# The Silu gate of the mLSTM path moved behind the head-output transpose, with channels on partitions

## The chip, the cores and the metric

The kernel runs on one core of one Trainium2 chip. The metric is the device time in microseconds of one execution. Five engines of the core appear below: PE (TensorE, the matrix multiplier; PEld are its weight loads), DVE (VectorE), ACT (ScalarE), POOL (GpSimd) and SP (SyncE, which here only starts DMA transfers).

## The reference

One layer over 2048 tokens and 1024 model channels. RMSNorm, one input projection, two groups of heads, one output projection with a residual add, a final RMSNorm. The part that the change touches is the end of group A (4 heads of 256 channels):

```python
hm = mlstm_chunkwise(q, k, v, i_pre, f_pre)
hm = jax.nn.sigmoid(o_pre) * hm
hm = hm.reshape(B, S, N_HEADS, HEAD_DIM)
hm = hm * lax.rsqrt(jnp.mean(hm * hm, axis=-1, keepdims=True) + EPS)   # norm per token and head
hm = hm.reshape(B, S, D_MLSTM) * mh_norm_g                             # gain per channel
hm = hm * jax.nn.silu(z_m)                                             # gate per token and channel
mix = concatenate([hm, c])                    # c: convolution group, causal depthwise, width 31
h = h + einsum('bse,ed->bsd', mix, w_out)
```

So each element of the head output is multiplied by a factor of its token (the norm), a gain of its channel, and silu(z) of both. z = u W_z, where u is the normed input.

## The kernel before, in words

**Halves, units, heads, chunks.** The sequence is worked in two halves of 1024 tokens (`hf`). For each half the input projection is cut into *units* of 256 output channels. A unit is 8 steps over the 1024 input channels; every operand is split into a high and a low part, and three products (hh, hl, lh) are added, so that a unit is 8 x 3 products into four PSUM banks of the pool `gm` (five buffers). The units of a half come in this order: `g0, v0, g1, o0, z0, q0, k0`, then for each further head `g, g, v, o, z, q, k`, and at the end four `c` units. `g` feeds the convolution, `c` its gate, and `o`, `z`, `q`, `k`, `v` a head of the mLSTM.

**Two layouts of a unit.** Kind `fm` (L336) puts channels on partitions: the weights are the stationary operand, 512 tokens stream past, 96 matmuls of 512 columns. Kind `tm2` (L343) puts tokens on partitions: the activations are stationary, 256 channels stream, 192 matmuls of 256 columns. `q`, `k`, `g` and `c` are `fm`; `o`, `z` and `v` are `tm2`. What leaves PSUM must be multiplied by the norm factor of its token: in `tm2` a column `rstd["c"]` with one value per partition, in `fm` a row `rstd["b"]` of 512 values.

**Evacuation.** For each of the four banks of a `z` unit, and for each of its two token blocks, ACT takes a sigmoid (L450) and DVE multiplies it by the scaled value (L451): silu(z) with tokens on partitions, stored in `oz` beside the sigmoid of `o` (L438).

**The chunk chain.** After unit `k` of a head, `mlstm(hf, h)` puts that head's 8 chunks of 128 tokens into slots, one slot per step of the following units. A chunk has four parts. `s0`: `sk` on PE (scores and transposed k, in the only buffer of PSUM pool `tp`), `w` and `kw` on DVE and ACT, `qs` on DVE. `s1`: `num` on PE, state update `kv` on PE and `cs` on DVE, the denominator `dn` and `hm` (L694) on DVE, the sum of squares on ACT (L699), its power on POOL (L700). `s2`: second half of the state update; `hm` times norm factor times silu(z) on DVE (L706). `s3`: transpose of `hm` on PE (`mt`, L714, in the same single buffer of `tp`), channel gain on ACT (L719), and a DMA of `mo` to DRAM every second chunk.

**Background work.** The convolution is 31 taps over 1024 tokens for each of 8 blocks (L777 and L787 on DVE), put between other work by a credit counter (`pump`). The LayerNorm of the convolution runs in four blocks per half, those of half 0 at the beginning of half 1. A block has two matmuls on PE in its chain: `lm` for the mean and `lv` for the variance, then `bc_l` (broadcast), with DVE and ACT between them. The convolution's input tiles `c` have two buffers, so the PSUM bank of a `g` unit's first part (L756) can leave only after the convolution two blocks before is done.

**What sets the order.** Each engine runs its queue in order. The order of the queues is not the order of the code: a scheduler lays the program out by priorities and by its own estimate of times, and only the instructions marked with `keep_in_program_order` (the taps, the exponentials) are fixed. A change of a few operations therefore shifts matmuls and vector instructions in many places.

Of the kernel before, what the change touches and what calls it, by code (L numbers as in the profile page):

```python
# [14 lines left out]
F32 = mybir.dt.float32  # L15
F32R = mybir.dt.float32r
AF = mybir.ActivationFunctionType
ALU = mybir.AluOpType

P = 128  # L20
# [4 lines left out]
HD = 256  # L25
# [14 lines left out]
def hybrid_block_kernel(  # L40
# [12 lines left out]
    nc = tc.nc  # L53
# [5 lines left out]
    PAD, ODD = 8, 48  # L59
# [56 lines left out]
    def col(base, i):  # L116
        return vec[:, base + i : base + i + 1]
# [259 lines left out]
                pump(step_us * PUMP)  # L377


    q_t, k_t, v_t, oz_t = {}, {}, {}, {}  # L380
    gate = {}

    def ev_q(hf, h):
# [49 lines left out]

    def ev_o(hf, h):
        def f(i, ps):
            oz_t[h, i] = ozp.tile([P, 2, 2, HD], F32, tag="oz", name=f"oz_{hf}_{h}_{i}")
            for j in range(2):
                nc.scalar.activation(  # L438
                    oz_t[h, i][:, 0, j], ps[:, j * HD : (j + 1) * HD], AF.Sigmoid,
                    scale=rstd["c"][:, 2 * i + j : 2 * i + j + 1],  # L440
                )
        return f

    def ev_z(hf, h):
        def f(i, ps):
            t = oz_t[h, i]
            for j in range(2):
                pv = ps[:, j * HD : (j + 1) * HD]
                rc = rstd["c"][:, 2 * i + j : 2 * i + j + 1]
                nc.scalar.activation(t[:, 1, j], pv, AF.Sigmoid, scale=rc)  # L450
                nc.vector.scalar_tensor_tensor(  # L451
                    out=t[:, 1, j], in0=pv, scalar=rc, in1=t[:, 1, j], op0=ALU.mult, op1=ALU.mult
                )
        return f

    def gates(hf, gt):
# [103 lines left out]
    def mlstm(hf, h):  # L560
# [46 lines left out]
        def chunk(c):  # L607
# [4 lines left out]
            sl = slice(cc * P, (cc + 1) * P)  # L612
            last = hf == 1 and c == NCH - 1
            v = [v_t[h, c // 2][:, i, c % 2, :] for i in range(2)]
            sg = oz_t[h, c // 2][:, 0, c % 2, :]
            sz = oz_t[h, c // 2][:, 1, c % 2, :]
            t = {}

            def s0():
# [83 lines left out]
            def s2():  # L703
                state(1)
                hm = t["hm"][:, :HD]
                nc.vector.scalar_tensor_tensor(  # L706
                    out=hm, in0=hm, scalar=t["ss"], in1=sz, op0=ALU.mult, op1=ALU.mult
                )

            def s3():  # L710
                hm = t["hm"]
                mt = tp.tile([P, 512], F32, tag="tp", name=f"mt_{nm_}")
                for d in range(2):
                    nc.tensor.transpose(mt[:, d * P : (d + 1) * P], hm[:, d * P : (d + 1) * P], ident)  # L714
                if cc % 2 == 0:
                    dec["mo"] = k2p.tile([P, 2, 256], F32, tag="k2", name=f"mo_{nm_}")
                mo = dec["mo"]
                for d in range(2):
                    nc.scalar.activation(  # L719
                        mo[:, d, (cc % 2) * P : (cc % 2 + 1) * P], mt[:, d * P : (d + 1) * P],  # L720
                        AF.Identity, scale=col(V_MG, 2 * h + d),
                    )
                if cc % 2 == 1:
                    nc.sync.dma_start(
                        mixs[2 * hf + tb][:, 2 * h : 2 * h + 2, (cc - 1) * P : (cc + 1) * P], mo
                    )
# [194 lines left out]
    for hf in range(2):  # L921
        s = [("g", 0)]
        for h in range(NH):
            s += [("v", h)] + ([("g", 1)] if h == 0 else []) + [("o", h), ("z", h), ("q", h), ("k", h)]
            if h < 3:
                s += [("g", 2 * h + 2), ("g", 2 * h + 3)]
        s += [("c", j) for j in range(4)]
        seq.append(s)
        for u in s:
            if u == ("v", 0):  # L930
                for _ in range(2):
                    for g in range(2):
                        wsrc.append((wv0[g], 528, 0))
            else:
                for g in range(2):
                    wsrc.append((wu[WID[u], g], 512, ODD if u[0] in "ozv" else 0))
    for b in range(4):
        for nn in range(2):
            for g in range(8):
# [18 lines left out]
    for hf in range(2):  # L958
# [8 lines left out]
        for ui, (nm, i) in enumerate(s):  # L967
# [10 lines left out]
            if nm == "g":  # L978
                unit("fm", 8, 2, 256, opnd, ev_glu(hf, i), hook=hook)
            elif nm == "c":  # L980
                unit("fm", 8, 2, 256, opnd, ev_zc(hf, i), hook=hook)
            elif nm == "q":
                unit("fm", 8, 2, 256, opnd, ev_q(hf, i), hook=hook)
            elif nm == "k":
                unit("fm", 8, 2, 256, opnd, ev_k(hf, i), hook=hook)
                mlstm(hf, i)
            elif nm == "o":
                unit("tm2", 8, 2, 256, opnd, ev_o(hf, i), hook=hook)
            elif nm == "z":
                unit("tm2", 8, 2, 256, opnd, ev_z(hf, i), hook=hook)  # L990
            elif i > 0:
                unit("tm2", 8, 2, 256, opnd, ev_v(hf, i), hook=hook)
            else:
                for g in range(2):
                    unit("tm", 8, 2, 264, opnd, ev_v0(hf, g, gt), step_us=1.35, toks=[4 * g + i for i in range(4)])
                gq.append([0, gates(hf, gt)])
                gate_step()
# [129 lines left out]
```

## Time and profile before

| | |
|---|---|
| median of 3 runs | 2007.02 us (2005.82 to 2014.35) |
| the profiled execution's own time | 2014.07 us |
| its span in the profile | 2012.4 us |
| PE busy | 1975.9 us, 98% |
| DVE busy | 1445.4 us, 72% |
| ACT busy | 827.7 us, 41% |
| POOL busy | 792.3 us, 39% |
| granted PE clock, mean | 0.993 |

The profiled execution is one of the slower ones, 7 us above the median. PE is nearly always busy, so the first question is what each stretch of PE costs; the second is where PE does wait, and for whom. Busy time is an average: DVE's 72% is made of stretches near 95% and of a last fifth of the span below 35%. Rows of the trace that carry the argument stand in a section below. In them `start us, us` is the start and the length of a run of equal instructions; an entry in brackets is the idle time of the engine before it and who ended it. The four projections by layout: L336 is `fm`, L343 is `tm2`, L350 is the output projection and the first `v` unit.

### The profile page before, as it was taken

How to read it: one execution, taken by the hardware profiler on the slowest of the kernel's cores; microseconds unless marked ns; L12 is line 12 of the kernel's file. 1: busy time of each engine (PE TensorE's matmuls, PEld its weight loads, DVE VectorE, ACT ScalarE, POOL GpSimd, SP SyncE). 2: the span in 40 equal slices, each digit the busy share in tenths (PEclk: the TensorE clock that was granted, in tenths of full speed). 3: DMA queues.
4: the chain of work that ended last, by engine and by line, in shares of the span. 5: the costliest groups of instructions: out<-in, count | busy, mean ns of one | idle time of the engine just before them, and what ended most of it. 6: DMA issues, size and time to landing. Idle time of an engine off the chain costs nothing.

```text
span 2012.4 us, 29602 instructions
## 1 busy us (share of the span) xinstructions
PE 1975.9 (98%) x11562; PEld 1744.7 (87%) x11562; DVE 1445.4 (72%) x1915; ACT 827.7 (41%) x1703; POOL 792.3 (39%) x740
## 2 busy tenths in 40 slices
PE   8999999999999999999999999999999999999998
PEld 7998998899899888888889879988998887788887
DVE  6598887699679765557799998977896658733221
ACT  5233432442343246545345224424523555543332
POOL 4632432333243332433333324333432236565564
PEclk9999999999999999999999999999999999999999
DMA  4121121212122233335211211211221566766452
GB/s 151 64 69 53 58 74 43 63 49 74 42 69 74 74 110 125 113 126 162 85 53 53 69 42 59 74 53 53 64 74 53 163 220 200 248 231 231 155 190 95
DMA packets 85836, 204.10 MB, mean 101 GB/s; under 512 B 7296, under 2 KB 40256, under 8 KB 85696
## 3 DMA queue, kind: packets, MB, share of 16 engines
q1 hardware_dynamic: 85696, 202.21, 30.6%
q8 instruction: 91, 1.49, 0.3%
q14 instruction: 49, 0.40, 0.1%
HBM read 159.15 MB, written 43.03 MB: 100 GB/s over the span
## 4 chain that ended last, share of the span: by engine, by line
PE 73%; DVE 18%; DMA 3%; issue 2%; ACT 2%; POOL 0%; SPq 0%; POOLq 0%; DVEq 0%; ACTq 0%
PE gm L336 32%; PE gm L343 18%; PE gm L350 16%; DVE y L787 11%; PE num L601 3%; PE kv L601 2%; PE sk L627 1%; DMA ly<-ysc 1%; DVE sm L302 1%; DMA wr<-in_wo 1%; PE mt L714 1%; DVE ly L844 1%; DMA ysc<-y 1%; PE sk L631 1%; ACT ly L881 0%
## 5 line engine op out<-in xcount | busy, mean ns | idle before, releaser
L222 POOL TENSOR_TENSOR w<-wr,w 128x512 fp32r<-128x512 f32 (+1 forms) x392 | 603.1, 1543 | 878.2 <-ACT w L221 859.4
L336 PE MATMUL gm<-u_u,w 128*128 128x512 f32 x3840 | 908.6, 392 | 0.7 <-DVE u_u L293 0.6
L336 PEld LDWEIGHTS gm<-u_u,w 128*128 128x128 f32 x3840 | 712.5, 188 | 143.2 <-DVE u_u L293 1.3
L787 DVE SCALAR_TENSOR_TENSOR y<-c,vec,y 128x1024 f32<-128x1024 f32 x480 | 714.5, 1489 | 9.7
L343 PE MATMUL gm<-w,u_u 128*128 128x256 f32 x4224 | 521.9, 281 | 5.7 <-DVE oz L451 3.4
L343 PEld LDWEIGHTS gm<-w,u_u 128*128 128x128 f32 x4224 | 505.8, 190 | 7.6 <-DVE oz L451 3.6
L221 ACT CAST w<-wr 128x512 fp32r<-128x512 f32 (+1 forms) x392 | 241.4, 620 | 591.6 <-PE gm L336 200.2
L350 PE MATMUL gm<-w,u_m 128*128 128x512 f32 x1536 | 355.0, 392 | 3.1 <-POOL w L222 1.9
L350 PEld LDWEIGHTS gm<-w,u_m 128*128 128x128 f32 x1536 | 289.1, 189 | 64.2 <-POOL w L222 2.8
L281 DVE TENSOR_TENSOR u_m<-mr,u_m 128x1024 fp32r<-128x1024 f32 x32 | 47.2, 1475 | 77.7 <-ACT u_m L280 77.7
L1019 DVE TENSOR_TENSOR ht<-gm,ht 128x512 f32<-128x512 f32 x32 | 21.5, 687 | 112.2 <-PE gm L350 112.2
L700 POOL TENSOR_TENSOR ss<-ss,nhalf 128x1 f32<-128x1 f32 x64 | 55.5, 867 | 111.9 <-ACT sq L699 111.3
L633 DVE SCALAR_TENSOR_TENSOR w<-sk,rs,ee 128x128 f32<-128x128 f32 x64 | 22.0, 344 | 81.6 <-PE sk L631 79.1
L601 PE MATMUL kv<-v,kw 128*128 128x258 f32 x360 | 74.3, 291 | 0.6 <-DVE cs L666 0.4
L666 DVE SCALAR_TENSOR_TENSOR cs<-cs,g_so,kv 128x258 f32<-128x258 f32 x112 | 53.3, 476 | 25.1 <-PE kv L601 24.7
L639 ACT ACTIVATE kw<-sk,g_wa 128x256 fp32r<-128x256 f32 x60 | 28.3, 472 | 81.7 <-DVE w L633 81.6
L719 ACT ACTIVATE mo<-mt,vec 128x128 f32<-128x128 f32 x128 | 39.7, 362 | 52.3 <-PE mt L714 52.1
L601 PEld LDWEIGHTS kv<-v,kw 128*128 128x128 f32 x360 | 56.9, 190 | 3.2 <-DVE cs L666 0.6
L408 DVE SCALAR_TENSOR_TENSOR v<-gm,rs,v 128x256 fp32r<-128x256 f32 x64 | 29.5, 475 | 33.4 <-ACT v L407 33.4
L699 ACT ACTIVATE sq<-hm 128x257 bf16<-128x257 f32 x64 | 26.9, 420 | 64.6 <-DVE hm L694 64.4
L761 POOL TENSOR_TENSOR c<-c,g 128x512 f32<-128x512 f32 x32 | 40.9, 1284 | 30.4 <-ACT g L760 27.6
L350 PE MATMUL gm<-w,u_u 128*128 128x264 f32 x384 | 50.8, 294 | 0.0
(200 smaller groups left out, 1818.0 us busy)
## 6 DMA issues: line engine op xcount, KB each, us to landing
wr<-in_wu SPq DMA_DIRECT2D x123, 512.0 KB, 3.6
wr<-in_wo SPq DMA_DIRECT2D x64, 512.0 KB, 3.6
mr<-mixs SPq DMA_DIRECT2D x32, 512.0 KB, 4.6
ysc<-y SPq DMA_DIRECT2D x16, 512.0 KB, 2.6
mixs<-mo SPq DMA_DIRECT2D x32, 256.0 KB, 2.1
zsc<-zc SPq DMA_DIRECT2D x32, 256.0 KB, 2.1
ly<-ysc SPq DMA_DIRECT2D x16, 512.0 KB, 5.2
lz<-zsc SPq DMA_DIRECT2D x16, 512.0 KB, 6.0
```

What stands on the lines that cost most here:

```text
L221: nc.scalar.copy(hi, s)
L222: nc.gpsimd.tensor_tensor(out=lo, in0=s, in1=hi.bitcast(F32), op=ALU.subtract)
L281: nc.vector.tensor_tensor(out=l_, in0=src, in1=h_.bitcast(F32), op=ALU.subtract)
L336: nc.tensor.matmul(ps[i], wt[:, o + cb * P : o + (cb + 1) * P], at[:, tb * 512 : (tb + 1) * 512], start=st, stop=sp_,)
L343: nc.tensor.matmul(ps[i][:, t2 * 256 : (t2 + 1) * 256], at[:, t * P : (t + 1) * P], wt[:, o : o + ncol], start=st and t2 == 0, stop=sp_, s ...
L350: nc.tensor.matmul(ps[i][:, :ncol], at[:, t * P : (t + 1) * P], wt[:, o : o + ncol], start=st, stop=sp_,)
L601: nc.tensor.matmul(ps, x_, y_, start=start and i == 0, stop=stop and i == 2)
L666: nc.vector.scalar_tensor_tensor(out=cs[:, d], in0=cs[:, d], scalar=so[:, h, c : c + 1], in1=kv[:, :VW], op0=ALU.mult, op1=ALU.add,)
L700: nc.gpsimd.tensor_tensor(out=ss, in0=ss, in1=nhalf[:, 0:1], op=ALU.pow)
L719: nc.scalar.activation(mo[:, d, (cc % 2) * P : (cc % 2 + 1) * P], mt[:, d * P : (d + 1) * P], AF.Identity, scale=col(V_MG, 2 * h + d),)
L761: nc.gpsimd.tensor_tensor(out=c[:, sl], in0=c[:, sl], in1=g, op=ALU.mult)
L787: tc.keep_in_program_order(nc.vector.scalar_tensor_tensor(out=y, in0=c[:, j + i * H2 : j + (i + 1) * H2], scalar=col(V_CW, b * CW + j), in1=y,
```

## The change

`z` becomes an `fm` unit: 96 matmuls of 512 columns in place of 192 of 256. Its four banks are each left by one DVE multiplication with the row of norm factors (new L451) and one ACT Silu in SBUF (new L452). The tiles of `o` and `z` are separated; there are again four buffers, two for `o` and two for `z` of a head. In the chunk, `s2` is now an ACT scaling by the norm factor of the token (new L705, an Identity activation with a scale per partition), and `s3` multiplies gain and silu(z) on DVE as the transposed head output leaves PSUM (new L716, two instructions of 128 columns). The weights of `z` lose their 48-element offset in the weight tile.

```diff
-    q_t, k_t, v_t, oz_t = {}, {}, {}, {}
+    q_t, k_t, v_t, o_t, z_t = {}, {}, {}, {}, {}
...
     def ev_o(hf, h):
         def f(i, ps):
-            oz_t[h, i] = ozp.tile([P, 2, 2, HD], F32, tag="oz", name=f"oz_{hf}_{h}_{i}")
+            if i % 2 == 0:
+                o_t[h, i // 2] = ozp.tile([P, 4, HD], F32, tag="oz", name=f"o_{hf}_{h}_{i // 2}")
             for j in range(2):
                 nc.scalar.activation(
-                    oz_t[h, i][:, 0, j], ps[:, j * HD : (j + 1) * HD], AF.Sigmoid,
+                    o_t[h, i // 2][:, 2 * (i % 2) + j], ps[:, j * HD : (j + 1) * HD], AF.Sigmoid,
                     scale=rstd["c"][:, 2 * i + j : 2 * i + j + 1],
                 )
...
     def ev_z(hf, h):
         def f(i, ps):
-            t = oz_t[h, i]
-            for j in range(2):
-                pv = ps[:, j * HD : (j + 1) * HD]
-                rc = rstd["c"][:, 2 * i + j : 2 * i + j + 1]
-                nc.scalar.activation(t[:, 1, j], pv, AF.Sigmoid, scale=rc)
-                nc.vector.scalar_tensor_tensor(
-                    out=t[:, 1, j], in0=pv, scalar=rc, in1=t[:, 1, j], op0=ALU.mult, op1=ALU.mult
-                )
+            cb, tb = i % 2, i // 2
+            if cb == 0:
+                z_t[h, tb] = ozp.tile([P, 2, 512], F32, tag="oz", name=f"z_{hf}_{h}_{tb}")
+            t = z_t[h, tb][:, cb, :]
+            nc.vector.tensor_tensor(out=t, in0=ps, in1=rstd["b"][:, tb * 512 : (tb + 1) * 512], op=ALU.mult)
+            nc.scalar.activation(t, t, AF.Silu)
         return f
...
-            sg = oz_t[h, c // 2][:, 0, c % 2, :]
-            sz = oz_t[h, c // 2][:, 1, c % 2, :]
+            sg = o_t[h, tb][:, cc, :]
+            sz = z_t[h, tb][:, :, sl]
...
             def s2():
                 state(1)
                 hm = t["hm"][:, :HD]
-                nc.vector.scalar_tensor_tensor(
-                    out=hm, in0=hm, scalar=t["ss"], in1=sz, op0=ALU.mult, op1=ALU.mult
-                )
+                nc.scalar.activation(hm, hm, AF.Identity, scale=t["ss"])
...
                 for d in range(2):
-                    nc.scalar.activation(
-                        mo[:, d, (cc % 2) * P : (cc % 2 + 1) * P], mt[:, d * P : (d + 1) * P],
-                        AF.Identity, scale=col(V_MG, 2 * h + d),
+                    nc.vector.scalar_tensor_tensor(
+                        out=mo[:, d, (cc % 2) * P : (cc % 2 + 1) * P], in0=mt[:, d * P : (d + 1) * P],
+                        scalar=col(V_MG, 2 * h + d), in1=sz[:, d], op0=ALU.mult, op1=ALU.mult,
                     )
...
-                    wsrc.append((wu[WID[u], g], 512, ODD if u[0] in "ozv" else 0))
+                    wsrc.append((wu[WID[u], g], 512, ODD if u[0] in "ov" else 0))
...
             elif nm == "z":
-                unit("tm2", 8, 2, 256, opnd, ev_z(hf, i), hook=hook)
+                unit("fm", 8, 2, 256, opnd, ev_z(hf, i), hook=hook)
```

The scheduler moves instructions on every engine. Three places in the queues follow. They all lie at the start of half 1: the four LayerNorm blocks of half 0, then the first convolution blocks and the chunks of head 0. In the names the second number of `num_0_2` is the chunk, the last number of a name only tells equal names apart.

**PE, the variance matmul of the last LayerNorm block** (`lv_3`; `gm_0_9560` and `gm_x_904x` belong to unit `k0`). Before:

```order
L336 MATMUL gm_2_9431<-u_u_7_8131,w_9433 128x512 x3
L336 MATMUL gm_3_9432<-u_u_7_8131,w_9433 128x512 x3
L336 MATMUL gm_0_9560<-u_u_0_7963,w_9464 128x512
L859 MATMUL lv_3_9181<-invd,lq_3_0_9068 128x1 x2
L336 MATMUL gm_0_9560<-u_u_0_7963,w_9464 128x512 x2
```

Now, in the changed kernel:

```order
L336 MATMUL gm_1_9041<-u_u_6_7680,w_9044 128x512 x2
L336 MATMUL gm_2_9042<-u_u_0_7547,w_8944 128x512 x3
L336 MATMUL gm_2_9042<-u_u_1_7577,w_8944 128x512
L336 MATMUL gm_3_9043<-u_u_0_7547,w_8944 128x512 x3
L856 MATMUL lv_3_8751<-invd,lq_3_0_8652 128x1 x2
L336 MATMUL gm_2_9042<-u_u_1_7577,w_8944 128x512 x2
```

`lv_3` stood behind the first matmul of unit `k0`; it now stands behind 51 of its 96 (24 into the first bank, 20 into the second, 4 and 3 into the others).

**PE, chunks 2 and 3 of head 0** (`gm_3_10009` is the last bank of the unit `g3`). Before:

```order
L601 MATMUL num_0_2_10025<-c1h_0_1_9963,qssl_0_2_9955 128x258
L336 MATMUL gm_3_10009<-u_u_0_7963,w_9762 128x512 x3
L336 MATMUL gm_3_10009<-u_u_1_7993,w_9762 128x512 x3
L336 MATMUL gm_3_10009<-u_u_2_8012,w_9854 128x512 x3
L336 MATMUL gm_3_10009<-u_u_3_8034,w_9854 128x512 x3
L336 MATMUL gm_3_10009<-u_u_4_8053,w_9921 128x512 x3
L336 MATMUL gm_3_10009<-u_u_5_8077,w_9921 128x512 x3
L627 MATMUL sk_0_3_10070<-q_0_0_9554,k_0_0_9685 128x128 x2
L631 MATMUL sk_0_3_10070<-ident,k_0_0_9685 128x128 x2
L601 MATMUL kv_0_2_1_10091<-v_0_1_8417,kw_0_2_9944 128x258 x3
L336 MATMUL gm_3_10009<-u_u_6_8096,w_10010 128x512 x3
```

Now:

```order
L600 MATMUL num_0_2_9505<-c1h_0_1_9443,qssl_0_2_9435 128x258
L626 MATMUL sk_0_3_9550<-q_0_0_9034,k_0_0_9165 128x128 x2
L630 MATMUL sk_0_3_9550<-ident,k_0_0_9165 128x128 x2
L600 MATMUL kv_0_2_1_9571<-v_0_1_8001,kw_0_2_9424 128x258 x3
L600 MATMUL num_0_3_9618<-v_0_1_8001,wsh_0_3_9560 128x258 x2
L600 MATMUL kv_0_3_0_9628<-v_0_1_8001,kw_0_3_9557 128x258 x2
L711 MATMUL mt_0_2_9599<-ident,hm_0_2_9528 128x128 x2
```

Before, the matmuls of the last bank of `g3` and the beginning of the next unit lay between `sk` and `num` of chunk 3; now nothing but the three `kv` matmuls does, and that bank of `g3` comes after them.

**DVE, the same place** (`y` are taps of the convolution; `w_0_3` comes from `sk` of chunk 3). Before:

```order
L787 SCALAR_TENSOR_TENSOR y_0_9330<-c_0_8280,vec,y_0_9330 128x1024
L592 TENSOR_TENSOR qssl_0_2_9955<-qs_0_2_9952,qssh_0_2_9954 128x256
L756 TENSOR_TENSOR c_2_9994<-gm_2_9707,rb_8138 128x512
L756 TENSOR_TENSOR c_2_9994<-gm_0_9705,rb_8138 128x512
L666 SCALAR_TENSOR_TENSOR cs_0_9691<-cs_0_9691,g_so_9227,kv_0_2_0_10035 128x258
L687 TENSOR_SCALAR dn_0_2_10044<-num_0_2_10025,g_en_9223 128x1
L690 TENSOR_TENSOR dn_0_2_10044<-dn_0_2_10044,num_0_2_10025 128x1
L592 TENSOR_TENSOR c0l_0_2_10041<-cs_0_9691,c0h_0_2_10040 128x258
```

Now:

```order
L591 TENSOR_TENSOR qssl_0_2_9435<-qs_0_2_9432,qssh_0_2_9434 128x256
L716 SCALAR_TENSOR_TENSOR mo_0_0_9352<-mt_0_1_9461,vec,z_0_0_8899 128x128 x2
L665 SCALAR_TENSOR_TENSOR cs_0_9171<-cs_0_9171,g_so_8785,kv_0_2_0_9515 128x258
L784 SCALAR_TENSOR_TENSOR y_0_8852<-c_0_7864,vec,y_0_8852 128x1024
L686 TENSOR_SCALAR dn_0_2_9524<-num_0_2_9505,g_en_8781 128x1
L591 TENSOR_TENSOR c0l_0_2_9521<-cs_0_9171,c0h_0_2_9520 128x258
L665 SCALAR_TENSOR_TENSOR cs_0_9171<-cs_0_9171,g_so_8785,kv_0_2_1_9571 128x258
L784 SCALAR_TENSOR_TENSOR y_0_8852<-c_0_7864,vec,y_0_8852 128x1024
L689 TENSOR_TENSOR dn_0_2_9524<-dn_0_2_9524,num_0_2_9505 128x1
L591 TENSOR_TENSOR c1l_0_2_9577<-cs_0_9171,c1h_0_2_9576 128x258
L784 SCALAR_TENSOR_TENSOR y_0_8852<-c_0_7864,vec,y_0_8852 128x1024
L690 RECIPROCAL dn_0_2_9524<-dn_0_2_9524 128x1
```

The product `mo`, which leaves PSUM from the transpose, is new on DVE. Behind the last row shown follow a tap, `hm`, a tap and then `w_0_3`: five taps lie between `mo` of chunk 1 and `w` of chunk 3, and the two evacuations `c_2`, which free banks for `g3`, come five rows behind `w_0_3`. Before, `c_2` stood ahead of that.

## Rows read from the trace of the kernel before

**Rows 1.** The page's chain of work that ended last, by engine and by line.

```profile
PE 73%; DVE 18%; DMA 3%; issue 2%; ACT 2%; POOL 0%; SPq 0%; POOLq 0%; DVEq 0%; ACTq 0%
PE gm L336 32%; PE gm L343 18%; PE gm L350 16%; DVE y L787 11%; PE num L601 3%; PE kv L601 2%; PE sk L627 1%; DMA ly<-ysc 1%; DVE sm L302 1%; DMA wr<-in_wo 1%; PE mt L714 1%; DVE ly L844 1%; DMA ysc<-y 1%; PE sk L631 1%; ACT ly L881 0%
```

**Rows 2.** Windows: stretch, length; busy PE, PEld, DVE, ACT, POOL; clock, DMA.

```profile
300.00:400.00 100.00, 100.00 (x512) 85.26 (x511) 72.43 (x92) 33.72 (x72) 31.52 (x28) 1.00 0.19 58
...
976.00:1244.00 268.00, 256.67 (x1536) 227.14 (x1535) 252.21 (x324) 103.10 (x231) 94.13 (x87) 0.98 0.18 58
```

**Rows 3.** Windows of three z units, L343 alone: PE, PEld, clock.

```profile
285.83:307.75 21.92, 21.85 (x193) 21.65 (x192) 1.00 0.22 73
460.50:483.28 22.78, 22.76 (x194) 22.56 (x192) 1.00 0.21 70
...
906.00:937.30 31.30, 27.13 (x195) 25.74 (x194) 0.89 0.54 167
```

**Rows 4.** The same for one fm unit, L336 alone.

```profile
504.90:526.82 21.92, 21.92 (x98) 18.20 (x97) 1.00 0.16 49
```

**Rows 5.** PE in order of time, inside the z unit of half 1, head 0.

```profile
928.26 5.92 PE L343 MATMUL gm<-w,u_u 128*128 128x256 f32 x26 [3.42 <-DVE oz L451]
```

**Rows 6.** The window after that wait, as rows 2.

```profile
927.60:934.40 6.80, 6.14 (x29) 6.14 (x29) 2.41 (x6) 1.22 (x3) 1.28 (x1) 0.50 0.61 206
```

**Rows 7.** PE in order of time, lv_3 within unit k0 of half 1.

```profile
961.27 0.50 PE L859 MATMUL lv<-invd,lq 128*128 128x1 f32 x4
```

**Rows 8.** DVE in order of time, from lv_3 to the first chunks.

```profile
961.81 0.16 DVE L861 TENSOR_SCALAR lrs<-lv 128x2 f32<-128x2 f32 x1 [3.69 <-PE lv L859]
...
975.88 1.79 DVE L777 TENSOR_SCALAR y<-c,vec 128x1024 f32<-128x1024 f32 x1
977.71 15.00 DVE L787 SCALAR_TENSOR_TENSOR y<-c,vec,y 128x1024 f32<-128x1024 f32 x10
...
1025.39 0.48 DVE L694 SCALAR_TENSOR_TENSOR hm<-num,dn,oz 128x256 f32<-128x256 f32 x1
...
1060.01 0.22 DVE L687 TENSOR_SCALAR dn<-num,g_en 128x1 f32<-128x1 f32 x1 [0.72 <-PE num L601]
```

**Rows 9.** DVE by line and form: count, busy, mean ns, idle before, releaser.

```profile
L706 DVE SCALAR_TENSOR_TENSOR hm<-hm,ss,oz 128x256 f32<-128x256 f32 x64 | 36.6, 573 | 13.0 <-POOL ss L700 12.8
...
L451 DVE SCALAR_TENSOR_TENSOR oz<-gm,rs,oz 128x256 f32<-128x256 f32 x64 | 27.3, 476 | 2.4 <-ACT oz L450 2.1
...
L633 DVE SCALAR_TENSOR_TENSOR w<-sk,rs,ee 128x128 f32<-128x128 f32 x64 | 22.0, 344 | 81.6 <-PE sk L631 79.1 <-ACT sq L699 1.6 <-ACT ee L623 0.7
...
L807 DVE TENSOR_TENSOR zc<-gm,rb 128x512 f32<-128x512 f32 x32 | 21.3, 685 | 4.2 <-PE gm L336 2.0 <-DMA zsc<-zc 2.0
```

**Rows 10.** ACT by line and form.

```profile
L719 ACT ACTIVATE mo<-mt,vec 128x128 f32<-128x128 f32 x128 | 39.7, 362 | 52.3 <-PE mt L714 52.1
...
L450 ACT ACTIVATE oz<-gm,rs 128x256 f32<-128x256 f32 x64 | 27.9, 478 | 37.6 <-PE gm L343 23.4 <-DVE oz L451 14.2
...
L808 ACT ACTIVATE zc<-zc 128x512 f32<-128x512 f32 x32 | 19.2, 626 | 5.6 <-DVE zc L807 4.1 <-issue 1.4
...
L760 ACT ACT_TABLE_LOAD x13 | 16.7, 1283 | 2.1 <-DVE g L759 1.9
```

**Rows 11.** ACT in order of time, around a table load.

```profile
892.60 1.28 ACT L881 ACT_TABLE_LOAD   x1
893.90 4.05 ACT L881 ACTIVATE ly<-ly,vec 128x256 f32<-128x256 f32 x8
```

**Rows 12.** POOL by line, the power of the norm factor.

```profile
L700 POOL TENSOR_TENSOR ss<-ss,nhalf 128x1 f32<-128x1 f32 x64 | 55.5, 867 | 111.9 <-ACT sq L699 111.3
```

**Rows 13.** PE in order of time, waits in the stretch of rows 2.

```profile
998.78 0.39 PE L601 MATMUL num<-c0h_i,qssl 128*128 128x258 f32 x1 [0.90 <-DVE qssl L592]
...
1016.07 0.28 PE L601 MATMUL num<-c1h,qssl 128*128 128x258 f32 x1
...
1191.44 0.58 PE L601 MATMUL num<-c0h_i,qssl 128*128 128x258 f32 x1 [2.46 <-DVE qssl L592]
```

## The prediction

> **What bounds the kernel now.** I read the chain that ended last first. 73% of it is PE, most of that the three projection lines; 18% is DVE, and the largest share of that, 11%, is the taps of the convolution [rows 1]. So PE bounds the kernel, except in some stretch where the taps do. The windows say where. In an ordinary stretch (300 to 400) PE is busy for all 100 us and DVE for 72. From 976 to 1244 DVE is busy for 252.21 of 268 us, PE for 256.67 [rows 2]: both are nearly full, and which of them is late decides what a change is worth there. In order of time DVE starts its first tap at 975.88, and from then on it runs taps without a wait; the `num` matmul of a chunk starts at 1016.07 and lasts 0.28 us, and `hm`, which reads it, starts on DVE at 1025.39, 9 us later [rows 8, 13]. PE waits in this stretch are short and end with DVE (0.90 and 2.46 us, the shortest and the longest of those that I use) [rows 13]. I take DVE as the bound from 976 to 1244, and PE outside it.
>
> I then read PE's own cost of the units. A `z` unit in `tm2` takes 21.92 us in one window and 22.78 in another [rows 3]; four units (at 460, 635, 1290 and 1465) have the longer form. An `fm` unit takes 21.92 [rows 4]. The `z` unit of half 1, head 0 is a case of its own: its window is 31.30 us, at a mean clock of 0.89 [rows 3]. PE stands there for 3.42 us behind an evacuation on DVE [rows 5], and right after that wait 6.14 us of matmuls run at a clock of 0.50, which is 1.2 instead of 2.4 GHz [rows 6].
>
> **Part 1, z as an fm unit.** 96 matmuls of 512 columns replace 192 of 256. Seven of the eight units are ordinary. For the four longer ones PE gains 22.78 - 21.92 = 0.86 us each, for the others I take nothing. Two of the four lie before 976 and two after 1244: -1.7 and -1.7 us. The head-0 unit of half 1 should lose its 3.42 us wait, since its bank now leaves in one step of DVE that stands early in the queue and in front of ACT instead of behind it; with the wait the half clock goes, worth half of 6.14, so 3.07; and 0.86 as above. That is -7.35, with 0 as the other end (the evacuation again late behind other work of DVE).
>
> [...]
>
> **Part 2, evacuation.** Before, each bank costs DVE two instructions of 476 ns and ACT two of 478 [rows 9, 10]. Now DVE has one of 128x512 out of PSUM with a row, as the convolution gate does in 685 ns, and ACT one of 512 in SBUF, as that gate does in 626 [rows 9, 10]. Per unit DVE: 4 x 685 - 8 x 476 = -1.07 us; ACT: 4 x 626 - 8 x 478 = -1.3 us. ACT is hidden, being idle for 59% of the span, and for 165 of the 268 us in the dense stretch [rows 2].
>
> **Part 3, the chunk.** DVE loses `hm` x norm x silu, 573 ns [rows 9], and gets two products of 128x128 from PSUM. The nearest row is `w`, the same operation and shape from PSUM, 344 [rows 9]; as ends I keep 238 (half of the 256-column form) and 476. 2 x 344 - 573 = +115 ns a chunk (-97 to +379). ACT loses two instructions of 362 and gets one of 256 columns in SBUF, between 313 (half of the 512-column form) and 478 [rows 10]; at 420 it is 0.3 us lighter a chunk. The new wait: ACT's scaling needs the power from POOL, 867 ns [rows 12], for which DVE waited before. Behind it in ACT's queue stand mostly the high parts of `qs`, which lead to `num` on PE. If POOL were late each time, 64 x 0.87 = 56 us of ACT would stand; mostly an exponential and other casts lie between, and ACT has the room, so I cost it at nothing on the path, with 16 x 0.87 x a quarter = 3.5 us for the dense stretch as the upper end. PE now waits, for the single `tp` buffer, for DVE's products in place of ACT's: where DVE is late `mt` leaves later, and the next `sk` with it. DVE is in turn asked to wait for PE's `mt`. The one row of that kind shown is 0.72 us [rows 8]; I take +1 us for the dense stretch, 0 to 4.
>
> The dense stretch holds 16 chunks and one `z` unit: 16 x 0.115 - 1.07 = +0.8 us of DVE, +1 of waits, together +1.8.
>
> **Part 4, table loads.** ACT's queue holds 85 loads where it held 67, since Silu shares no table with its neighbours: 18 x 1.283 = 23.1 us on ACT [rows 10], hidden by the same idle time. After a load the next function starts 0.02 us later [rows 11].
>
> The Trainium skill speaks against this price: the page "ScalarE: Activation LUTs", section "What ACT_TABLE_LOAD costs", puts some 1380 ns of draining beside the 1283, 2.66 us a switch. By it 18 loads cost ACT 48 us. No drain is seen in the rows on either side of the load, so the trace does not agree; the forecast would be the same by both.
>
> **Part 5, the moved matmul.** This is the largest term. The last LayerNorm block of half 0 has its variance `lv_3` on PE; DVE waited 3.69 us for it and went on at 961.81 [rows 7, 8], then did the block's chain and began the taps at 975.88 [rows 8]. In the changed queue `lv_3` stands behind 51 of the 96 matmuls of `k0`, where it stood behind one. 50 x 21.92/96 [rows 4] = +11.4 us later. What precedes it on PE is 1.7 + 7.35 us earlier. So the first tap should start at 975.88 - 9.05 + 11.4, some 2.4 us later than before, and with it the stretch that DVE sets. The gain of parts 1 and 2 ahead of 976 is thus spent. DVE's row of waits [rows 8] names nothing else it could do meanwhile, since the taps keep their order; at best a part of the 15.8 us in which DVE is idle within the dense stretch [rows 2] makes up for it, and I put the lower end there at a third, -5 us.
>
> **Sum.** -1.7 - 7.35 + 11.4 + 1.8 - 1.7 = +2.4 us. On the profiled execution's own 2014.07 that is 2016.5; that execution was 7.05 above the median of 2007.02, so the time that I name is 2007.02 + 2.4 = 2009.4. Its own range: down by the 5 us of idle and a further 3 if all other units gain 0.86; up by 7.35 if the wait in `z` comes back: 2001 to 2017.
>
> **Rival A, PE sets the dense stretch.** PE is busy for 256.67 us of it and DVE for less, 252.21 [rows 2]. If the taps catch up before 1244, the later `lv_3` costs nothing and PE keeps all it saved: -1.7 - 7.35 - 0.86 (head 1) - 1.7 = -11.6, so 1995.4. For it: the busy times. Against it: `hm` 9 us behind `num`, and waits of PE that end with DVE [rows 8, 13].
>
> **Rival B, slower: chunk 3 stands on PE.** In the changed queue only three `kv` matmuls lie between `sk` and `num` of chunk 3 of head 0, where the last bank of `g3` and the next unit lay before. Meanwhile DVE has some five taps of 1.5 us (15.00 for ten [rows 8]) and small steps up to `w_0_3`: PE would stand for about 9 us. After the 3.42 us wait PE ran at half clock and lost 3.07 [rows 5, 6]; here as much. If DVE has taps enough to work through while PE stands, the 9 us are slack of PE and cost nothing, which is why they are not in the sum. They decide from the point where DVE itself runs dry, because the next chunk's `w`, `dn` and `hm` come from the matmuls that stand: then nothing of either engine's work covers them. DVE's idle time in the stretch, 15.8 us, of which 0.72 is a wait of that kind [rows 2, 8], leaves that open. Then +12.1 on the forecast: 2021.5.
>
> **Rival C, table loads on the path.** If each of the 18 loads stood ahead of something that PE waits for, +23 us: 2032. ACT ends few of the waits and is idle for most of the dense stretch [rows 2], so this is unlikely.
>
> **How the numbers follow.** Forecast 0.56, A 0.22, B 0.18, C 0.04. A measurement of this kernel can tell about 0.5%, some 10 us, from no change: below 1997 is faster, above 2017 slower. The forecast's own range touches neither; A is faster, B and C are slower. Faster 0.22, same 0.57, slower 0.21. The range goes to A and B, 1995 to 2021.5, and leaves out C and the outer part of either.
>
> **What would show it.** Part 1: `z` units of 21.9 us in windows at full clock, and no wait of some 3 us in the one of half 1, head 0. Parts 2 and 3: new lines on DVE near 685 and 344 ns, on ACT near 626 and 420; an idle entry of the scaling released by POOL would show the new wait. Part 5: `lv_3` in the middle of `k0`, and the first long run of taps near 978; a first tap well before 975 would refute the term. DVE again over 94% busy between there and the end of head 1's units bears out the forecast; PE without waits and DVE with idle time there speak for A; a PE wait of some 9 us at `num` of chunk 3, with a clock of 0.50 behind it and the end of the stretch 12 us late, for B. It would be wrong altogether if the time left 2001 to 2017.

## The result, and the profile after

The changed kernel takes 2030.12 us (median of 6, 2027.06 to 2030.83), the kernel before 2008.53 in the same runs: a ratio of 1.0102, interval 1.0091 to 1.0113. That is 21.6 us slower. The forecast was 2009.4, and its range, 1995 to 2021.5, does not hold the time. Rival C, to which the prediction gave 0.04, had named 2032.

Where PE's time goes can be added up. The span is PE's busy time and the rest; of the busy time, half of what ran at a granted clock of 0.50 is lost (a stretch in the first 41 us, which both kernels have, is counted in). I compare with a second profile of the kernel before (it took 2007.04; the one of the rows ahead took 2014.07, and 6 of its 7 us more are such half clock).

| us | span | not busy | lost at half clock | the rest |
|---|---|---|---|---|
| before, second profile | 2005.3 | 36.1 | 6.5 | 1962.7 |
| changed | 2029.1 | 53.0 | 15.9 | 1960.2 |
| difference | +23.8 | +16.9 | +9.4 | -2.5 |

"Not busy" is the span less PE's busy time on the page (1969.2 and 1976.1). So PE's work did get cheaper, and waits, with the half clock behind them, cost ten times what was saved. Windows of the changed kernel, columns as in [rows 2]: the `z` unit of half 1, head 0; a stretch at half clock; the dense stretch from the first tap of half 1 to that of the fifth convolution block, and one at half clock inside it; then two of the later stretches at half clock.

```profile
905.70:929.30 23.60, 23.60 (x109) 19.50 (x108) 14.83 (x18) 11.27 (x21) 8.71 (x5) 1.00 0.38 123
962.00:968.80 6.80, 4.92 (x12) 3.86 (x13) 2.17 (x4) 3.28 (x7) 0.00 (x0) 0.50 0.65 224
987.80:1262.70 274.90, 251.57 (x1451) 220.31 (x1450) 255.72 (x348) 108.35 (x225) 92.70 (x90) 0.98 0.18 57
1040.50:1047.30 6.80, 3.11 (x12) 2.98 (x13) 6.80 (x14) 4.02 (x10) 1.79 (x3) 0.50 0.37 118
...
1607.10:1610.50 3.40, 3.40 (x12) 2.66 (x11) 2.73 (x6) 0.63 (x1) 0.20 (x2) 0.50 0.80 277
1702.70:1706.10 3.40, 3.40 (x10) 2.73 (x10) 1.69 (x3) 1.24 (x3) 2.16 (x2) 0.50 0.78 274
```

The same in the second profile of before: the `z` unit, its half clock, the dense stretch.

```profile
905.90:935.50 29.60, 26.17 (x208) 25.84 (x207) 20.59 (x27) 14.66 (x26) 9.27 (x7) 0.94 0.53 172
927.80:931.20 3.40, 3.37 (x16) 3.37 (x17) 1.78 (x4) 0.36 (x1) 0.00 (x0) 0.50 0.95 334
974.30:1246.50 272.20, 260.25 (x1607) 230.69 (x1605) 257.83 (x341) 105.58 (x239) 96.78 (x91) 1.00 0.18 60
```

The `z` unit went from 29.60 to 23.60 us, at full clock. The dense stretch grew by 2.7 us only. But it begins at 987.8 in place of 974.3: 13.5 of the 23.8 us are there before its first tap. Where they come from stands on PE and DVE in order of time (what answers to [rows 7, 8, 13]):

```profile
959.58 1.19 PE L336 MATMUL gm<-u_u,w 128*128 128x512 f32 x4 [0.56 <-POOL w L222]
963.88 8.75 PE L336 MATMUL gm<-u_u,w 128*128 128x512 f32 x27 [3.10 <-ACT q L388]
972.47 0.50 PE L856 MATMUL lv<-invd,lq 128*128 128x1 f32 x4
...
1044.19 0.80 PE L600 MATMUL num<-v,wsh 128*128 128x258 f32 x2 [8.33 <-ACT wsh L590]
...
1606.79 0.39 PE L600 MATMUL num<-c0h,qssh 128*128 128x258 f32 x1 [1.93 <-ACT qssh L590]
```

```profile
973.01 0.16 DVE L858 TENSOR_SCALAR lrs<-lv 128x2 f32<-128x2 f32 x1 [8.48 <-PE lv L856]
...
987.77 1.78 DVE L774 TENSOR_SCALAR y<-c,vec 128x1024 f32<-128x1024 f32 x1
```

PE stood in unit `k0` for ACT's copies of `q`, ran at half clock, and came to `lv_3` at 972.47; DVE had waited 8.48 us for it. ACT in the same time, and before the later wait at 1606.79:

```profile
958.42 1.06 ACT L845 ACTIVATE lq<-ly 128x1024 f32<-128x1024 f32 x1 [2.23 <-DVE ly L841]
960.64 1.06 ACT L845 ACTIVATE lq<-ly 128x1024 f32<-128x1024 f32 x1 [1.17 <-DVE ly L841]
961.72 1.28 ACT L550 ACT_TABLE_LOAD   x1
963.01 0.23 ACT L550 ACTIVATE g_wa<-g_wa 128x32 f32<-128x32 f32 x1
963.15 0.21 ACT L550 ACTIVATE g_so<-g_so 128x32 f32<-128x32 f32 x1
963.26 2.02 ACT L388 COPY q<-gm 128x512 f32<-128x512 f32 x4
...
1601.45 1.28 ACT L647 ACT_TABLE_LOAD   x1
1602.75 0.40 ACT L647 ACTIVATE nm<-nm,g_bc 128x128 f32<-128x128 f32 x1
1603.17 1.28 ACT L805 ACT_TABLE_LOAD   x1
1604.46 0.63 ACT L805 ACTIVATE zc<-zc 128x512 f32<-128x512 f32 x1
```

The copies of `q`, a unit that PE left at 953.1, stand behind two squares of the LayerNorm that wait for DVE, then a table load. Behind the loads at 1601.45 and 1603.17 the cast `qssh` comes late for `num`. ACT is idle for 59% of the span here too; its queue is short of order, not of time. The new lines by form:

```profile
L705 ACT ACTIVATE hm<-hm,ss 128x256 f32<-128x256 f32 x64 | 32.5, 507 | 46.5 <-POOL ss L699 46.4
L622 ACT ACT_TABLE_LOAD x22 | 28.2, 1283 | 0.4
L757 ACT ACT_TABLE_LOAD x19 | 24.4, 1283 | 2.2 <-DVE g L756 1.9
L452 ACT ACTIVATE z<-z 128x512 f32<-128x512 f32 x32 | 19.0, 626 | 34.4 <-DVE z L451 34.4
...
L452 ACT ACT_TABLE_LOAD x7 | 9.0, 1283 | 0.1
```

```profile
L716 DVE SCALAR_TENSOR_TENSOR mo<-mt,vec,z 128x128 f32<-128x128 f32 x128 | 39.0, 344 | 28.5 <-PE mt L711 28.0
L451 DVE TENSOR_TENSOR z<-gm,rb 128x512 f32<-128x512 f32 x32 | 20.4, 681 | 2.7 <-PE gm L336 2.7
```

In the kernel before:

```profile
L623 ACT ACT_TABLE_LOAD x13 | 16.7, 1283 | 0.2
...
L450 ACT ACT_TABLE_LOAD x2 | 2.6, 1283 | 0.0
```

Of the 18 loads more, 7 - 2 = 5 stand at Silu itself; in front of the exponential of `ee` there are 22 for 13 and at the convolution's sigmoid 19 for 13 [rows 10]; the other lines together hold two fewer. So most come from ACT's new order, in which exponentials and sigmoids alternate more often, and not from Silu, the reason that the prediction gave.

### The profile page after: what moved, and what is told of

Its sections match the earlier page's. It is cut to its first block, busy times and chain, and to the rows that moved or that the text cites. A ratio compares the mean times of both kernels' runs of the same rounds, so it can differ in the third digit from the quotient of the medians.

```text
span 2029.1 us, 27952 instructions
## 1 busy us (share of the span) xinstructions
PE 1976.1 (97%) x10794; PEld 1712.0 (84%) x10794; DVE 1431.9 (71%) x1947; ACT 833.9 (41%) x1625; POOL 802.1 (40%) x740
## 5 line engine op out<-in xcount | busy, mean ns | idle before, releaser
L336 PE MATMUL gm<-u_u,w 128*128 128x512 f32 x4608 | 1088.5, 393 | 7.0 <-ACT q L388 3.1
L336 PEld LDWEIGHTS gm<-u_u,w 128*128 128x128 f32 x4608 | 857.4, 189 | 181.8 <-ACT q L388 3.5
L222 POOL TENSOR_TENSOR w<-wr,w 128x512 fp32r<-128x512 f32 (+1 forms) x392 | 613.3, 1570 | 859.7 <-ACT w L221 812.3
L343 PE MATMUL gm<-w,u_u 128*128 128x256 f32 x2688 | 337.8, 281 | 7.3 <-DVE g L756 3.4
L343 PEld LDWEIGHTS gm<-w,u_u 128*128 128x128 f32 x2688 | 323.4, 189 | 9.1 <-DVE g L756 3.6
L590 ACT CAST c0h<-cs 128x258 fp32r<-128x258 f32 x56 | 22.8, 408 | 115.9 <-DVE cs L665 110.2
L716 DVE SCALAR_TENSOR_TENSOR mo<-mt,vec,z 128x128 f32<-128x128 f32 x128 | 39.0, 344 | 28.5 <-PE mt L711 28.0
L705 ACT ACTIVATE hm<-hm,ss 128x256 f32<-128x256 f32 x64 | 32.5, 507 | 46.5 <-POOL ss L699 46.4
```

The lines of the kernel that those rows point to most:

```text
L222: nc.gpsimd.tensor_tensor(out=lo, in0=s, in1=hi.bitcast(F32), op=ALU.subtract)
L336: nc.tensor.matmul(ps[i], wt[:, o + cb * P : o + (cb + 1) * P], at[:, tb * 512 : (tb + 1) * 512], start=st, stop=sp_,)
L343: nc.tensor.matmul(ps[i][:, t2 * 256 : (t2 + 1) * 256], at[:, t * P : (t + 1) * P], wt[:, o : o + ncol], start=st and t2 == 0, stop=sp_, s ...
L716: nc.vector.scalar_tensor_tensor(out=mo[:, d, (cc % 2) * P : (cc % 2 + 1) * P], in0=mt[:, d * P : (d + 1) * P], scalar=col(V_MG, 2 * h + d ...
```

## The experiments

Each group of medians stands with the kernel before, measured beside it.

**The kernel before once more.** 

> The kernel before, unchanged, profiled once more. The execution profiled first took 2014, the other five 2006 to 2011. If the wait of 3.42 us in the z unit of half 1, head 0 and the half clock behind it are what made that one longer, an execution near 2008 shows that unit at 23 to 26 us in place of 31.1, and then the change had nothing to win there. If the wait belongs to the kernel, the unit is 31 us again and the 6 us lie elsewhere.


2007.04; the unit is 29.60 us, with its wait, 3.43 us against 3.42 [rows 5]:

```profile
927.83 4.82 PE L343 MATMUL gm<-w,u_u 128*128 128x256 f32 x26 [3.43 <-DVE oz L451]
```

The wait belongs to the kernel. 1.7 us of the first profile's extra are in this unit, whose half clock lasted 6.8 us there and 3.4 here; the rest is half clock elsewhere.

**One part at a time, and one function.** (`stt` is short for `scalar_tensor_tensor`; the diffs of this section are shortened.)

```diff
 z_only:      s2  -ACT Identity(hm, scale=ss)      +DVE stt(hm * ss * sz)
              s3  -DVE stt(mt * gain * sz)         +ACT Identity(mt, scale=gain)
 chunk_only:  before, with s2, s3 of the changed kernel
 sigmoid:     -nc.scalar.activation(t, t, AF.Silu)  +... AF.Sigmoid   (ev_z)
```

> The z part alone: z as an fm unit with Silu, but the chunk as before (DVE multiplies hm by norm and gate in one step, ACT applies the gain out of PSUM). The gate is read in the wrong layout, so the values are wrong; the work is the same. Its queue has lv_3 behind 51 matmuls of k0 and nothing of a unit between sk and num of chunk 3, as in the changed kernel. Theory 1 (the z part's new order of the queues carries the loss): 2024 to 2032, lv_3 near 972, first tap near 988, PE idle 8 us at num of chunk 3. Theory 2 (the products mo on DVE, in the way of the single tp buffer, carry it): 2000 to 2010. Theory 3 (table loads): 75 loads in the queue where the changed kernel has 85 and the kernel before 67, so about 2017.

> The chunk part alone: z in tm2 with sigmoid and product as before; s2 scales by the norm on ACT, s3 multiplies gain and gate on DVE out of PSUM (gate read in the wrong layout, values wrong, work the same). Its queue has lv_3 behind one matmul of k0 and 24 matmuls between sk and num of chunk 3, as the kernel before. Theory 1: 2004 to 2013. Theory 2: 2020 to 2030. Theory 3: 79 loads against 67, so about 2022.

> The changed kernel with Sigmoid in place of Silu in the z evacuation (so z times its sigmoid is left out; the values are wrong). PE's queue is the same as in the changed kernel, ACT's has 79 table loads in place of 85. Theories 1 and 2: within 2 us of the changed kernel's 2030. Theory 3 (table loads on the path): 6 loads fewer of 18 more, so some 7 us faster, 2022 to 2024.

Before 2007.28. z_only 2015.82 (ratio 1.0037, 1.0025 to 1.0048), chunk_only 2023.26 (1.0078, 1.0059 to 1.0097), sigmoid 2029.68. Theory 1 fails: the chunk part alone loses 16 us. Theory 2 fails: the `z` part alone loses 8.5 us. Theory 3 is near with both, but seems to fail with sigmoid, which took away 6 loads for nothing. Of the 18 loads more, 12 are already in chunk_only, which has no Silu in `z`. The traces say more. In z_only the first tap is at 984.7, 10.4 us late, and that lateness stays: the dense stretch takes 272.9 us, as before. In chunk_only it is at 976.3, but the dense stretch takes 283.9 us, and DVE's waits there end with ACT for 16.4 us against 3.7 before. ACT and DVE of chunk_only in such a place:

```profile
1055.03 0.51 ACT L706 ACTIVATE hm<-hm,ss 128x256 f32<-128x256 f32 x1 [1.08 <-POOL ss L700]
1055.45 0.46 ACT L639 ACTIVATE kw<-sk,g_wa 128x256 fp32r<-128x256 f32 x1
1055.80 0.28 ACT L591 CAST wsh<-w 128x128 fp32r<-128x128 f32 x1
1056.11 1.28 ACT L648 ACT_TABLE_LOAD   x1
1057.40 0.40 ACT L648 ACTIVATE nm<-nm,g_bc 128x128 f32<-128x128 f32 x1
```

```profile
1055.93 0.48 DVE L640 SCALAR_TENSOR_TENSOR kw<-sk,g_wa,kw 128x256 fp32r<-128x256 f32 x1 [0.69 <-ACT kw L639]
1056.33 0.28 DVE L592 TENSOR_TENSOR wsl<-w,wsh 128x128 fp32r<-128x128 f32 x1
1057.83 0.42 DVE L651 TENSOR_TENSOR qs<-q,nm 128x256 f32<-128x256 f32 x1 [1.22 <-ACT nm L648]
```

Two candidates stand in one picture: ACT waits 1.08 us for POOL's power, and a load stands before the exponential that DVE waits 1.22 us for.

**ACT's wait for POOL, and the copies of q.**

```diff
 chunk_pool:    -nc.scalar.activation(hm, hm, AF.Identity, scale=t["ss"])
                +nc.gpsimd.tensor_scalar(out=hm, in0=hm, scalar1=t["ss"], scalar2=None, op0=ALU.mult)
 z_qdve, after_qdve (ev_q, hf == 1 and h == 0):  -nc.scalar.copy  +nc.vector.tensor_copy
 after_pool_q:  both, on the changed kernel
```

> The chunk part alone as in chunk_only, but the scaling by the norm factor is done by POOL, right behind the power that it waits for, so that ACT's queue has no instruction any more that waits for POOL. (Gate read in the wrong layout, as there.) Theory A (ACT stands behind POOL's power, and what lies behind it, kw, the exponentials and the high parts, comes late to DVE, which bounds this stretch): DVE's idle time released by ACT between the first tap of half 1 and the fifth convolution block falls from 16 us to some 4, and the time from 2023 to 2009 to 2014. Theory B (the two products on DVE, later in the order, hold the single tp buffer and so the next sk): 2021 to 2025 as before.

> The z part alone as in z_only, but in half 1, head 0 the four banks of q leave through DVE instead of ACT. Theory A (the first tap is late because unit k0 stands 3.1 us for ACT's copies of q and then runs at half clock, with the variance matmul behind it): no wait in k0, the first tap at 976 to 979 in place of 984.7, and the time from 2015.8 to 2006 to 2010. Theory B (the 7.45 us that PE stands at chunk 3, and the half clock there, are the cost): 2014 to 2018, with the same standing in chunk 3.

> The changed kernel, with q of half 1, head 0 through DVE. Theory A: the first tap at 979 to 981 in place of 987.8. If the loss of the chunk part (16 us alone) is of its own, it shows now: 2020 to 2025. If the changed kernel loses only by the late first tap, the time falls by 7 to 10 us and no more is left: 2019 to 2022 with a dense stretch no longer than 276 us. Theory B (standing at chunk 3): 2028 to 2031.

> The changed kernel with both: q of half 1, head 0 through DVE, and the scaling by the norm on POOL. Theory A (the late first tap, and ACT behind POOL, make up the loss): 2003 to 2012. Theory B (standing at chunk 3, products on DVE): 2022 or more.

Before 2008.10. chunk_pool 2023.14, z_qdve 2013.83, after_qdve 2022.44, after_pool_q 2029.54. Theory A fails for chunk_pool and after_pool_q. Without its wait for POOL the chunk part is as slow as with it. That alone does not clear the wait: the order of the queues changed too (the first tap is 4.6 us later than in chunk_only, the dense stretch 2.6 us shorter), and POOL's own 1148 ns for the step may hide a gain. z_qdve lies within the error of z_only, its first tap at 984.6, not at 976 to 979. Taking `q` off ACT shortened PE's wait (1.14 in place of 3.10) and the time by 8 us on the changed kernel, but the first tap stayed at 986.8: in the new order `lv_3` stood 10 matmuls later still, and ran at 969.86. Most of the gain, 5.4 us, lies behind the dense stretch, where it was not expected, and in after_pool_q, with its first tap at 990.1, none of it is left.

**No table loads.**

```diff
 before_sq, chunk_sq, after_sq:  -AF.Sigmoid  -AF.Silu  +AF.Square   (everywhere)
```

> The kernel before with Square in the place of every Sigmoid and Silu (the gates are left out; the work of each instruction is the same), so that ACT's queue holds 2 table loads in place of 67. PE's queue is unchanged. Theory T (loads stand in front of exponentials and casts that DVE and PE wait for): some us faster than before, 1998 to 2004, most of it in the dense stretch, which holds 13 loads. Theory O (only the order of the queues counts): 2005 to 2010.

> chunk_only with Square in the place of every Sigmoid and Silu: 2 table loads in place of 79, PE's queue unchanged. In the trace of chunk_only DVE stood 16 us for ACT between the first tap of half 1 and the fifth block, and of the waits over 1 us most ended with an exponential or a cast right behind a table load. Theory T: the time comes within 5 us of before_sq (2000 to 2008). Theory O: 2017 to 2023, some 15 us above before_sq.

> The changed kernel with Square in the place of every Sigmoid and Silu: 2 table loads in place of 85, PE's queue unchanged. Theory T alone: within 5 us of before_sq. Theory O alone: 20 to 24 us above it. Both (the late first tap is of the order, the rest of the loads): 8 to 14 us above before_sq, with a first tap 8 us or more later than there.

Before 2007.92. before_sq 2005.69 (0.9977, 0.9966 to 0.9988), chunk_sq 2001.90 (0.9965, 0.9952 to 0.9977), after_sq 2009.99 (1.0008, 0.9997 to 1.0019). In the traces each kernel has the order of its original on PE, DVE, ACT and POOL, and Square takes ACT as long as what it replaces (626 ns in `ev_z`, as before). So only the loads are gone, nearly all of them and not the 18 alone. The chunk part falls by 21 us, the changed kernel by 20, the kernel before by 2. Theory T holds, and wholly for the chunk part, which without loads is 4 us faster than the kernel before without loads; and as it still waits 57.1 us for POOL in all, that wait is not the cause:

```profile
L706 ACT ACTIVATE hm<-hm,ss 128x256 f32<-128x256 f32 x64 | 32.6, 510 | 57.7 <-POOL ss L700 57.1
```

after_sq stays 4.3 us above before_sq. Its first tap is 9.1 us later than there, but the dense stretch, first of before_sq, then of after_sq, is 4.4 us shorter, though PE stands at chunk 3 as in the changed kernel:

```profile
969.70:1242.60 272.90, 262.52 (x1609) 232.81 (x1609) 257.94 (x341) 89.15 (x226) 95.33 (x91) 0.99 0.18 59
```

```profile
978.80:1247.30 268.50, 249.25 (x1443) 218.33 (x1442) 254.87 (x347) 84.55 (x207) 92.92 (x89) 0.97 0.18 58
```

```profile
1034.22 0.80 PE L600 MATMUL num<-v,wsh 128*128 128x258 f32 x2 [8.32 <-ACT wsh L590]
```

**The LayerNorm's matmuls earlier.**

```diff
-        push(0.1, mean)
+        push(0.1, fast(mean))      # fast: fn() under tc.high_priority(offset=HP)
-        push(0.6, var)
+        push(0.6, fast(var))
```

> The changed kernel with a higher priority for the two steps of the LayerNorm that hold its matmuls. lv_3 stands 5.5 us of PE work earlier, and 28 matmuls of a unit lie between sk and num of chunk 3 instead of none; the rest of PE's queue moves little. Theory O: first tap at 979 to 983 in place of 987.8, no standing of 8 us at chunk 3, and 2018 to 2024. If the late first tap costs nothing: 2027 to 2031.


2019.96 (1.0048, 1.0033 to 1.0063). PE and DVE of after_ln:

```profile
960.96 0.50 PE L856 MATMUL lv<-invd,lq 128*128 128x1 f32 x4
...
1034.12 7.93 PE L336 MATMUL gm<-u_u,w 128*128 128x512 f32 x24 [4.09 <-DVE c L753]
```

```profile
975.80 1.79 DVE L774 TENSOR_SCALAR y<-c,vec 128x1024 f32<-128x1024 f32 x1
```

The first tap is 12 us earlier, at the place of before, and the time 10 us shorter. PE no longer stands for `q`, nor 8 us at chunk 3; it stands 4.09 us for a `g` bank instead.

**Fewer loads with all functions kept.**

```diff
 decay(tb):  +for cc in range(4): Exp(ee[:, cc]); Exp(nm[:, cc])   (kept in order)
 s0():       -Exp(ee[:, cc])   -Exp(nm[:, cc])
```

> The kernel before with the exponentials of four chunks issued together, one behind the other, when their inputs arrive, instead of one or two in each chunk. The same instructions, but ACT's queue changes table 45 times in place of 67. By what the Square runs showed (65 loads fewer were worth 2 us in the kernel before): 2003 to 2009, as before within the error. If exponentials that come early or late matter by themselves, the time moves by more than 5 us.

> The changed kernel with the exponentials of four chunks together: 52 table loads in place of 85, all functions kept, PE's queue nearly unchanged (lv_3 in the same place, nothing of a unit between sk and num of chunk 3). Theory T (of the 22 us lost some 18 are table loads that stand in front of what DVE waits for): most of the loads in the dense stretch go, and 2012 to 2019 is reached; DVE's idle time ended by ACT in the dense stretch falls from 11 us to 6 or less. If only Square itself was faster (not the loads): 2027 to 2031.

> The same with the priority of after_ln for the LayerNorm's matmuls (lv_3 5.5 us of PE work earlier, 24 matmuls between sk and num of chunk 3): both causes lessened. If they add, 2003 to 2011, at the level of the kernel before or a little better; if they are the same microseconds counted twice, 2012 to 2019 as after_grp.

Before 2007.63. before_grp 2010.07 (1.0013, 1.0002 to 1.0023), after_grp 2019.74 (1.0049, 1.0031 to 1.0066), after_grp_ln 2009.83 (1.0007, 0.9998 to 1.0016). 33 loads fewer are worth 10 us on the changed kernel; 22 fewer are worth nothing on the kernel before, which is 2.4 us slower with them, 1 us outside what was expected. With the earlier LayerNorm matmuls as well the loss is 2.2 of 21.6 us, not clear of the noise, and the two add. But the gain of after_grp isn't where it was expected: the dense stretch is 276.6 us, no shorter, and DVE's waits for ACT there (5.2 us against 11.1) are replaced by waits for PE. It lies behind: by the starts of PE's units, after_grp gains 8.5 us on the changed kernel between 1303 and 1782, where the wait of 1.93 us at 1606.79 and those of the last LayerNorms, with their half clock, are gone.

**Almost no loads.**

```diff
 tanh_ln (after_ln), tanh_grp_ln (after_grp_ln):
-Sigmoid(x)   +Tanh(x / 2), then Identity(bias=1)     (o, z, g; 0.5 in steps that were there; z's product on POOL)
```

> after_ln with all functions kept, but the gates of o, z and the convolution by Tanh (sigmoid as 0.5 + 0.5 tanh of half the argument, the addition by one more ACT instruction, the product for z on POOL, the factors 0.5 in steps that were there). ACT's queue holds 21 table loads in place of 83, since Tanh and Exp need no load between them; ACT has 128 more instructions. Theory T: the loads' part of the loss goes on top of what after_ln won: 2002 to 2010, at or below the kernel before. If it is ACT's work that counts and not the loads: 2018 or more.

> The same with the exponentials of four chunks together: 11 table loads. If loads are what is left, a few us below tanh_ln; if only the number of loads in the way of the chunk chain counted, within 3 us of it, as few are left there. 2000 to 2010.

Before 2008.68. tanh_ln 2014.10 (1.0026, 1.0016 to 1.0036), tanh_grp_ln 2020.70 (1.0060, 1.0047 to 1.0072). The first is 6 us better than after_ln, 4 us short of what was expected; the second misses it by 11, though it has 11 loads where after_grp_ln has 52. So the number of loads is no price. tanh_grp_ln has a wait on PE that the profile puts down to ACT; but ACT had itself been idle for 16.14 us until DVE's `w`, which stood behind 14 taps, so this wait is the order's:

```profile
1197.98 0.80 PE L620 MATMUL num<-v,wsh 128*128 128x258 f32 x2 [5.74 <-ACT wsh L610]
```

```profile
1197.27 0.47 ACT L655 ACTIVATE kw<-sk,g_wa 128x256 fp32r<-128x256 f32 x1 [16.14 <-DVE w L649]
```

```profile
1177.61 19.37 DVE L801 SCALAR_TENSOR_TENSOR y<-c,vec,y 128x1024 f32<-128x1024 f32 x14
1196.89 0.34 DVE L649 SCALAR_TENSOR_TENSOR w<-sk,rs,ee 128x128 f32<-128x128 f32 x1
```

Its first tap is at 984.4, not 976.8 as in after_grp_ln. Whether the added ACT steps or the order that came with them cost the time wasn't taken apart. No version beat the kernel before with all functions kept.

## Why the prediction was wrong

**The step that failed is part 4**, 18 loads priced at nothing because ACT has idle time. The count was right (85), though Silu accounts for 5 of the 18 only, and so was the duration (1283 ns). But a load sits in a queue in order, before an exponential or a cast that DVE or PE waits for, and idle time elsewhere does not hide that: by the starts of PE's units, after_sq wins 3.9 us around the wait at 1606.79 and its half clock alone. Without loads the loss falls from 21.6 to 4.3 us, so 17.3 go; with 33 fewer and all functions kept, 10. These are prices of loads in the changed order, old and new together; the share of the 18 new ones was not separated. Rival C had the mechanism and, by 18 x 1.283 = 23.1, nearly the size. That agreement is partly luck: six loads fewer in sigmoid, in the same order, gave nothing, and the time is lost in a few places, as waits of DVE in the dense stretch or as waits of PE, some with a half clock behind them. The Trainium skill, page "ScalarE: Activation LUTs", section "What ACT_TABLE_LOAD costs", puts a drain of some 1380 ns beside each load. The trace does not agree: the exponential starts 0.01 us behind the load (1057.40), as in [rows 11], and the load 0.03 us behind the cast.

**Part 5** was right in its term and wrong in its sum. `lv_3` did move by 11.4 us of PE's work. What came on top was PE's wait of 3.10 us for `q` in the same unit, and 6.8 us of clock at 0.50, 4.92 of them busy: `lv_3` ran at 972.47, not 963.6, and the first tap came at 987.77, not 978. The prediction looked at what stands ahead of `lv_3` on PE, and not at what stands ahead of the bank evacuations on ACT. A part of this is part 4 again: a load stands at 961.72 in front of those copies, and without loads the first tap is 9.1 us late in place of 13.5. That such lateness is paid in full, since the dense stretch is DVE's, was borne out by two runs: z_only began its taps 10.4 us late and has a span 10.0 us longer, and after_ln, 12 us earlier, won 10 back. In after_sq about half of it was made up within the dense stretch.

**Part 1** held: the head-0 unit lost its wait and its half clock, 6.0 us against the 7.35 forecast (its half clock was 3.4 us long in the second profile, not 6.8), and the four longer units gained 0.81 to 0.85 us each by their starts, against 0.86.

**Parts 2 and 3** held in their durations: 681, 626 and 344 ns; L705 took 507 against an upper end of 478. The wait for POOL is there, 46.4 us in all, and chunk_sq, which keeps it, loses nothing. The dense stretch is 2.7 us longer, against 1.8 in the sum; that is luck, as with the loads taken from both kernels it is 4.4 us shorter.

**Rival B** came in part: PE did stand 8.33 us at chunk 3, with a half clock that began within the wait. DVE was busy all through that window (6.80 of 6.80 us from 1040.50), so it fell into slack, as the forecast had said; after_sq keeps 8.32 us of it and has the shorter dense stretch. It wasn't taken away alone; after_ln removed it with the late tap. **Rival A** did not occur. Behind the dense stretch, where the sum had -1.7, the changed kernel lost 7.6 us more (13.5 + 2.7 = 16.2 at its end, 23.8 at the end of the span), and there after_grp won most.

The two parts lose 8.5 and 16.0 us alone and 21.6 together; why they don't quite add was not settled.

## What to carry to other kernels

Price an ACT table load by what stands behind it in ACT's queue and who waits for that, not by ACT's idle share; and after a change that puts a function on ACT, count how often the functions of different tables now alternate. Where several engines take turns, follow each moved instruction on the queue that feeds it too: the late matmul was only a part of the delay, the late evacuation another. Compare two profiles of the kernel before, before a single wait in one of them is put into a sum.

## What was not expected of the hardware

Waits of PE as short as 1.93 us (at 1606.79) were followed by 3.40 us of matmuls at a clock of 0.50. In the changed kernel 25 us of PE's busy time ran at that level, in seven stretches of 3.4 or 6.8 us, against 6.8 us in two before (the start left out); so 9.4 of the 23.8 us are clock. The length of a wait does not decide it: the wait of 3.42 us in the `z` unit of half 1, head 0 was followed by 6.8 us at 0.50 in the first profile [rows 6], by 3.4 in the second, and by none in before_sq:

```profile
925.44 3.23 PE L343 MATMUL gm<-w,u_u 128*128 128x256 f32 x26 [3.42 <-DVE oz L451]
```

```profile
925.40:932.20 6.80, 6.76 (x55) 6.67 (x56) 4.52 (x7) 2.31 (x5) 4.24 (x4) 1.00 0.57 186
```

A single profile's share of half clock is therefore in part chance.

With Tanh in place of Sigmoid, ACT needed no load between it and the exponential: 21 loads were left of 83.
